# A Pool memset after every fourth gather, in a gather, cumulative sum and projection kernel

## The chip, the cores and the metric

The kernel runs on one core of one Trainium2 chip. The metric is the device time in microseconds (us) of one execution. Medians of several executions are quoted, with the lowest and highest; a profiled execution gives the trace, whose span is 1.7 to 1.8 us shorter than the measured time of the same execution. A ratio is the mean time of one kernel's fast runs over the mean of the other's fast runs of the same rounds, so it is not quite the ratio of the medians quoted. A run counts as fast when it lies within 1.5% of the fastest run of its kernel.

In the lines of the profile PE is TensorE, PEld its weight loads, DVE VectorE, ACT ScalarE, POOL the GpSimd engine (Pool in this text) and SP SyncE. A record is the entry of one instruction in the trace. The landing time of a gather runs from its issue to the arrival of its data.

## The reference

```python
x: (16, 4096, 512) float32;  indices: (16, 2048), sorted, distinct;  w: (512, 512) float32
gathered = x[b_idx, indices, :]
cs = np.cumsum(gathered, axis=1)
return np.matmul(cs, w)            # (16, 2048, 512) float32
```

## The kernel before

The 16 x 2048 gathered rows are worked on as 256 tiles of 128 rows. For each tile the Pool issues one indirect DMA, which reads 128 rows of 2 KB and casts them to float16 on the way. TensorE multiplies the tile with a triangle of ones (four `sums` matmuls), VectorE adds the last row of the tile before (`carry`), TensorE projects with `w` (four `project` matmuls), ScalarE copies to SBUF, and SyncE stores four tiles, 1 MB, at a time. Buffers go round: sixteen gather tiles, four of most others. These are the lines that the change and the argument touch:

```python
    def gather(t):
        g, r = divmod(t, R)                       # R = 2
        if t % FREE == 0:                         # wait until an old gather tile has been summed
            pool.need(s_a, t + FREE - min(NG, 3 * R + max(t // (4 * R), 1) * R))
        ...                                       # ap: 128 row numbers, one per partition
        nc.gpsimd.indirect_dma_start(
            out=g16[g % (NG // R)][:, r, :], out_offset=None, in_=x_flat,
            in_offset=bass.IndirectOffsetOnAxis(ap=ap, axis=0),
            element_offset=(t // NT) * S * D,
        ).then_inc(s_g[t % NS], 16)
    ...
    for t in range(T):                            # T = 256, the whole program of the Pool
        gather(t)                                 # after a few fills at the start
    nc.gpsimd.drain()
    ...
    # in store(g, n): four tiles in one DMA
        nc.sync.dma_start(
            out=rows.rearrange(order, p=P, j=R), in_=src[:, g % W : g % W + n]
        ).then_inc(done, 16)
```

Of the kernel before, what the change touches and what calls it, by code (L numbers as in the profile page):

```python
# [7 lines left out]
P = 128  # L8
FP32 = mybir.dt.float32
FP16 = mybir.dt.float16  # L10
# [23 lines left out]
def kernel(  # L34
# [7 lines left out]
    nc = tc.nc  # L42

    B, S, D = x.shape
# [15 lines left out]
    NB = 4  # L60
# [10 lines left out]
    const = ctx.enter_context(tc.tile_pool(name="const", bufs=1))  # L71
# [10 lines left out]
    ident = const.tile([P, P], FP32)  # L82
    zeros = const.tile([P, D], FP16)
    spare = const.tile([P, 1], FP16)
    g16 = [const.tile([P, R, D], FP16, name=f"g16_{i}") for i in range(NG // R)]
    cst = [const.tile([P, DC, R, P], FP16, name=f"cst{i}") for i in range(NC)]
    ob = [const.tile([P, W, R, D], FP32, name=f"ob{i}") for i in range(NO)]
# [5 lines left out]
    def sem(name):  # L93
        return tc.alloc_semaphore(name)
# [5 lines left out]
    s_w = [sem(f"s_w{c}") for c in range(DC)]  # L100
    s_idx = [sem(f"s_idx{k}") for k in range(KI)]
    s_f = [sem(f"s_f{i}") for i in range(NO)]
    s_ol = sem("s_ol")
    s_g = [sem(f"s_g{i}") for i in range(NS)]
    s_o = [sem(f"s_o{i}") for i in range(NO)]
# [5 lines left out]
    pool, pe, dve, act, sp = (  # L111
        Lane(e) for e in (nc.gpsimd, nc.tensor, nc.vector, nc.scalar, nc.sync)
    )

    def gather(t):
        g, r = divmod(t, R)
        if t % FREE == 0:
            pool.need(s_a, t + FREE - min(NG, 3 * R + max(t // (4 * R), 1) * R))
        if t < FIRST:
            pool.need(s_first[g], 16)  # L120
            ap = idx_first[:, t, 0:1]
        else:
            pool.need(s_prep, t // P + 1)
            ap = idxg[:, t // P, t % P : t % P + 1]
        nc.gpsimd.indirect_dma_start(  # L125
            out=g16[g % (NG // R)][:, r, :],
            out_offset=None,
            in_=x_flat,
# [3 lines that stand above are left out]
# [93 lines left out]
    with nc.allow_non_contiguous_dma(reason="a few indices, one per partition"):  # L225
        for k, eng in enumerate((nc.sync, nc.scalar)):
            t = k * R
# [56 lines left out]
    ).then_inc(s_ut, 1)  # L284
    for t in range(T):
        gather(t)
    nc.gpsimd.drain()  # L287


# [124 lines left out]
```

## Time and profile before

| | value | how to read it |
|---|---|---|
| time | 354.61 us (354.37 to 355.48) | median of 3 runs |
| span of the profiled run | 352.6 us | all trace times count from its start |
| Pool | 69% busy | but 1.245 us from gather to gather, so nearly full |
| gather, issue to landing | 3.7 / 12.7 / 20.8 us | least, median, most: a queue in front of the DMA |
| last gather starts | 324.1 us | 28.5 us before the end of the span |

The lines themselves stand in the prediction.

### The profile page before, as it was taken

Reading aid. Unit: us, or ns where it says so; the run is one execution under the profiler, and the core shown is the slowest. Engines: PE = TensorE matmul, PEld = TensorE weight load, DVE = VectorE, ACT = ScalarE, POOL = GpSimd, SP = SyncE. Lnnn points to the kernel's source line nnn. Section 1 sums busy time; section 2 is a strip of 40 time slices with the busy share of each in tenths; the row PEclk is TensorE's granted clock in tenths of the full one; section 3 lists DMA queues with packets and bytes.
Section 4 is the critical chain, followed back from the end, with each engine's and each line's share of the span. In section 5 each row is a group of like instructions: output and inputs, shape, how many; then the busy total and the mean of one; then the engine's idle time right before and its main releaser. Section 6 shows DMA issues by size and latency. Waiting matters only on the chain.

```text
span 352.6 us, 6043 instructions
## 1 busy us (share of the span) xinstructions
PE 300.1 (85%) x2066; PEld 151.4 (43%) x2066; DVE 179.2 (51%) x263; ACT 152.7 (43%) x260; POOL 242.7 (69%) x266
## 2 busy tenths in 40 slices
PE   7687959889799898889979889889898988998983
PEld 2343525445344444444435444444444534443531
DVE  2554636555455455545546455455555545554531
ACT  2333525435344444444444445354444444444532
POOL 6777777777777777777777777777777767766000
PEclk9999999999999999999999999999999999999998
DMA  7999999999999999999999999999999999999996
GB/s 190 178 225 275 298 245 307 281 304 295 295 312 301 284 315 304 283 312 302 299 297 302 300 297 311 297 291 317 291 299 311 289 302 307 302 299 298 309 319 242
DMA packets 56315, 102.14 MB, mean 290 GB/s; under 512 B 5872, under 2 KB 38896, under 8 KB 56304
## 3 DMA queue, kind: packets, MB, share of 16 engines
q0 software_dynamic: 36864, 33.57, 58.9%
q1 hardware_dynamic: 18880, 67.90, 50.4%
q10 hardware_dynamic: 560, 0.53, 0.4%
q8 instruction: 6, 0.10, 0.1%
q14 instruction: 5, 0.04, 0.0%
HBM read 68.42 MB, written 67.11 MB: 384 GB/s over the span
## 4 chain that ended last, share of the span: by engine, by line
DMA 57%; POOL 23%; PE 9%; issue 9%; POOLq 0%; ACT 0%; SPq 0%
DMA g<-in_x_dram,idxg 56%; POOL g L125 23%; PE pb L190 6%; PE pa L145 3%; DMA idx_first<-in_indices_dram 1%; POOLq L287 0%; ACT ob L202 0%; SPq L409 0%; SPq L91 0%
## 5 line engine op out<-in xcount | busy, mean ns | idle before, releaser
L125 POOL DMA_INDIRECT g<-in_x_dram,idxg x252 | 237.2, 941 | 79.8 <-issue 64.3
L190 PE MATMUL pb<-w,cst 128*128 128x512 f16 x1024 | 262.3, 379 | 0.0
L177 DVE TENSOR_TENSOR cst<-pa,cst 128x512 f16<-128x512 f32 x240 | 166.1, 692 | 150.3 <-PE pa L145 148.5
L202 ACT COPY ob<-pb 128x512 f32<-128x512 f32 x256 | 150.1, 586 | 190.0 <-PE pb L190 190.0
L145 PE MATMUL pa<-ut,g 128*128 128x128 f16 x992 | 97.1, 220 | 43.1 <-DMA g<-in_x_dram,idxg 42.8
L145 PEld LDWEIGHTS pa<-ut,g 128*128 128x128 f16 x992 | 68.3, 98 | 123.6 <-DMA g<-in_x_dram,idxg 92.4
L190 PEld LDWEIGHTS pb<-w,cst 128*128 128x128 f16 x1024 | 89.5, 98 | 61.6 <-issue 0.5
L164 DVE CAST cst<-pa 128x512 f16<-128x512 f32 x16 | 11.1, 692 | 9.9 <-PE pa L145 9.9
L293 PE MATMUL pb<-zeros 128*128 128x512 f16 x16 | 5.7, 519 | 1.5 <-DVE zeros L297 1.5
L125 POOL DMA_INDIRECT g<-in_x_dram,idx_first x4 | 4.0, 989 | 1.6 <-issue 0.9
L145 PE MATMUL pa<-uq,g 128*128 128x128 f16 x32 | 3.1, 220 | 2.3 <-DMA g<-in_x_dram,idx_first 1.3
L145 PEld LDWEIGHTS pa<-uq,g 128*128 128x128 f16 x32 | 2.1, 98 | 4.8 <-DMA g<-in_x_dram,idxg 2.0
L293 PEld LDWEIGHTS pb<-zeros 128*128 128x128 f16 x16 | 1.9, 125 | 4.0 <-issue 2.0
L300 DVE CAST idxf<-idx 128x128 f32<-128x128 uint32 x2 | 0.5, 227 | 4.1 <-DMA idx<-in_indices_dram 4.1
L363 ACT ACT_TABLE_LOAD x1 | 1.3, 1283 | 2.5 <-issue 2.5
L366 ACT CAST w<-w 128x512 f16<-128x512 f32 x2 | 1.1, 614 | 2.6 <-DMA w<-in_w_dram 2.6
L314 DVE CAST w<-w 128x512 f16<-128x512 f32 x2 | 0.8, 451 | 1.2 <-DMA w<-in_w_dram 1.2
L305 PE MATMUL pb<-ident,idxf 128*128 128x128 f32 x2 | 0.7, 374 | 0.3 <-DVE idxf L300 0.3
L305 PEld LDWEIGHTS pb<-ident,idxf 128*128 128x128 f32 x2 | 0.4, 184 | 1.2 <-DVE idxf L300 0.9
L297 DVE MEMSET zeros<- 128x256 uint32 x1 | 0.3, 272 | 1.1 <-SPq L91 1.1
L311 DVE CAST idxg<-pb 128x128 uint32<-128x128 f32 x2 | 0.6, 288 | 0.2 <-PE pb L305 0.2
L253 POOL MEMSET ident<- 128x128 f32 x1 | 0.2, 205 | 0.5 <-SPq L91 0.5
(10 smaller groups left out, 1.9 us busy)
## 6 DMA issues: line engine op xcount, KB each, us to landing
out_dram<-ob SPq DMA_DIRECT2D x59, 1024.0 KB, 8.0
out_dram<-ob SPq DMA_DIRECT2D x8, 512.0 KB, 5.1
g<-in_x_dram,idxg POOLq DMA_INDIRECT x252, 12.8
out_dram<-ob SPq DMA_DIRECT2D x4, 256.0 KB, 3.3
w<-in_w_dram ACTq DMA_DIRECT2D x2, 256.0 KB, 3.7
w<-in_w_dram SPq DMA_DIRECT2D x2, 256.0 KB, 4.5
idx<-in_indices_dram SPq DMA_DIRECT2D x2, 128.0 KB, 3.2
g<-in_x_dram,idx_first POOLq DMA_INDIRECT x4, 4.2
```

The costliest lines, as they stand in the source:

```text
L125: nc.gpsimd.indirect_dma_start(out=g16[g % (NG // R)][:, r, :], out_offset=None, in_=x_flat, in_offset=bass.IndirectOffsetOnAxis(ap=ap, ax ...
L145: mm = nc.tensor.matmul(out=pa[t % NA][:, c], lhsT=g16[g % (NG // R)][:, r, c * P : (c + 1) * P], rhs=uq[:] if g in PLAIN else ut[:], star ...
L164: nc.vector.tensor_copy(out=dst, in_=src).then_inc(s_d, 1)
L177: nc.vector.tensor_tensor(out=dst, in0=src, in1=last, op=mybir.AluOpType.add).then_inc(s_d, 1)
L190: mm = nc.tensor.matmul(out=pb[u % NB][:], lhsT=cst[g % NC][:, c, j, :], rhs=w16[:, c, :], start=(c == 0), stop=(c == DC - 1),)
L202: nc.scalar.copy(out=ob[g // W % NO][:, g % W, j], in_=pb[u % NB][:]).then_inc(s_e, 1)
L293: nc.tensor.matmul(out=pb[NB - 1][:], lhsT=zeros[:, :P], rhs=zeros[:], start=True, stop=True)
L305: nc.tensor.transpose(out=pb[k % NB][:, :P], in_=idxf[:, k, :], identity=ident[:]).then_inc(s_pt, 1)
L311: nc.vector.tensor_copy(out=idxg[:, k, :], in_=pb[k % NB][:, :P]).then_inc(s_prep, 1)
L314: nc.vector.tensor_copy(out=w16[:, c, :], in_=w32[:, c, :]).then_inc(s_wc, 1)
L363: nc.scalar.copy(out=spare[:], in_=zeros[:, :1])
L366: nc.scalar.copy(out=w16[:, c, :], in_=w32[:, c, :]).then_inc(s_wc, 1)
```

## The change

The change is meant to give the Pool one more instruction per four gathers, about as long as a gather instruction, that nobody needs and that no other engine waits for. It shows what the Pool's time is worth in this kernel.

```diff
+    rest = const.tile([P, D * 3 // 2], FP16)
...
+    s_r = sem("s_r")
...
     for t in range(T):
         gather(t)
+        if t % NB == NB - 1:                      # NB = 4
+            pool.need(s_r, t // NB)
+            nc.gpsimd.memset(rest[:], 0.0).then_inc(s_r, 1)
     nc.gpsimd.drain()
```

The wait is for the memset before, four gathers earlier, since all of them write the same tile.

## The prediction

> **What bounds the kernel now.** I read the page of the kernel before first, then the line of the gathers by itself, then the chain that ended last in order of time, and last the Pool's own timeline at both ends of the run. The kernel takes 354.61 us (median); the profiled execution has a span of 352.6 us.
>
> From the page, the engine shares, the slices and the costliest lines:
>
> ```profile
> PE 300.1 (85%) x2066; PEld 151.4 (43%) x2066; DVE 179.2 (51%) x263; ACT 152.7 (43%) x260; POOL 242.7 (69%) x266
> ...
> POOL 6777777777777777777777777777777767766000
> ...
> DMA  7999999999999999999999999999999999999996
> ...
> DMA 57%; POOL 23%; PE 9%; issue 9%; POOLq 0%; ACT 0%; SPq 0%
> ...
> L125 POOL DMA_INDIRECT g<-in_x_dram,idxg x252 | 237.2, 941 | 79.8 <-issue 64.3
> ```
>
> The columns of the last line are busy us, mean ns, and the idle time in front. The Pool reads as 69% busy, but 252 gathers of 0.94 us with 79.8 us of idle in front make 317.0 us: it has almost no room. 64.3 us of that idle is put down to "issue", that is, to nothing the Pool waited for. The timeline in the middle of the run shows it as a fixed 0.30 us in front of each gather (columns: start, length, what, and idle before it):
>
> ```profile
> 156.72 0.94 POOL L125 DMA_INDIRECT g<-in_x_dram,idxg  x1 [0.30 <-issue]
> ...
> 157.97 0.94 POOL L125 DMA_INDIRECT g<-in_x_dram,idxg  x1 [0.30 <-issue]
> ...
> 159.22 0.94 POOL L125 DMA_INDIRECT g<-in_x_dram,idxg  x1 [0.30 <-issue]
> ```
>
> One gather costs the Pool 1.245 us from start to start, so 256 of them 318.8 us. The DMA is a little slower still. The view of the gathers' own line gives waits and landings:
>
> ```profile
>   issue: 65.2, 214
>   PE pa L145: 15.5, 41
> ...
> DMA to landing us min/median/max: 3.7/12.7/20.8
> ```
>
> The 41 waits for buffers total 15.5 us, of which 41 x 0.30 = 12.3 us is the fixed gap that a gather has anyway: only 3.2 us is true waiting. The landing time is the more telling line. The chain in order of time shows it rise all through the run, and the last gather comes last of all (columns: start, length, what):
>
> ```profile
> 12.25 5.50 DMA g<-in_x_dram,idxg
> ...
> 105.64 10.98 DMA g<-in_x_dram,idxg
> ...
> 230.21 16.99 DMA g<-in_x_dram,idxg
> ...
> 324.12 20.75 DMA g<-in_x_dram,idxg
> ```
>
> So the Pool issues at 1.245 us a tile, the DMA engines carry tiles (gather and store together) more slowly, and the difference lies as a queue in front of the DMA. The DMA's pace: first issue at 3.19, last landing at 324.12 + 20.75 = 344.87, so 341.7 us for 256 tiles, 1.335 us each. Pool and DMA are thus within 7% of each other: the DMA is the bound now, and the Pool's slack is 0.09 us a tile, some 0.36 us for four tiles, no more. From the last landing to the end of the span there are 352.6 - 344.87 = 7.7 us of tail (last sums, projection, copy, store).
>
> **What the Trainium skill says.** GPSIMD Engine Reference, section Instruction dispatch, says that each of the eight cores takes the next Pool instruction once its own share of the last is done, with no barrier between instructions. The trace agrees as far as it goes: the four one-element memsets at the start begin 0.03 us apart (0.31, 0.34, 0.37, 0.40) though each record lasts 0.10 to 0.12 us. The same page, section When to use GPSIMD, says that a pair of these cores writes the descriptors of a DMA issued there. Nothing in the trace of before shows which cores work; if it is so, a memset needs those two cores for its partitions too, and comes in series with the gathers on them. Perfetto Trace Analysis, section GPSIMD Engine Instruction, advises timing Pool instructions by the spacing of their starts and not by the reported duration; here that matters, 1.245 against 0.94 us. VectorE: DVE Perf Modes, section Zero memsets can be issued as uint32 (trn2), says that a memset costs a cycle per element whatever the type, and that a zero memset on VectorE may be issued in 4-byte words. The trace agrees: VectorE's zeros row has 128x256 uint32 for 512 halves, and on Pool 128 f16 take about what 128 f32 do.
>
> **The change part by part.** Nothing is removed or moved. Added are 64 Pool memsets of 128x768 f16, one behind each fourth gather, and in front of each (but the first) a wait for the memset before it, which four gathers (5 us) separate from it, so that wait should never hold. Nobody reads the tile; no engine but Pool gets work, and DMA traffic is the same.
>
> The cost of one memset, from these rows of the timeline at the start:
>
> ```profile
> 0.34 0.10 POOL L398 MEMSET const-float32-1.0<- 128x1 f32 x1
> ...
> 1.02 0.20 POOL L253 MEMSET ident<- 128x128 f32 x1 [0.51 <-SPq L91]
> 1.16 0.21 POOL L254 MEMSET ut<- 128x128 f16 x1
> ...
> 1.93 0.20 POOL L274 MEMSET uq<- 128x128 f16 x1
> ```
>
> One element has a record of 0.10 us and 128 elements one of 0.205: 0.105 / 127 = 0.83 ns an element. So 768 elements make 0.64 us and a record of 0.10 + 0.64 = 0.74 us, which is near enough to "about as long as a gather" (0.94). By start spacing, 128 elements hold the Pool for 0.14 us (1.02 to 1.16), that is 0.03 fixed and 0.11 for the elements; 768 then hold it for 0.03 + 0.64 = 0.67 us. Between two gathers the whole 0.67 and perhaps the 0.07 us until its writes are confirmed is added; I take 0.70 us.
>
> What lies beside other work: the Pool's slack of 0.36 us per four tiles is smaller than 0.70, so about half of each memset eats the DMA's queue, and from then on the Pool sets the pace at 1.245 + 0.70 / 4 = 1.42 us a tile, above the DMA's 1.335. The backlog that grows to 20.75 us never forms.
>
> The sum. Start of the first gather 3.19; extra length of the first gather and of the first with the computed indices, 0.19 + 0.15 (records 1.13 and 1.09); 255 periods of 1.245 = 317.5; 63 memsets of 0.70 before the last gather = 44.1. Last gather starts at 365.1. The same sum without memsets gives 320.9, plus 3.2 of buffer waits 324.1, as measured (324.12), which supports it. Those waits should vanish. The last landing with a short queue: the four first gathers took 4.2 us at the median, and some store traffic is beside it, so 6 us as a choice: 371.1. Tail 7.7: 378.8. The measured time stands 2.0 above the span (354.61 - 352.6): 380.8, taken as 381 us.
>
> **The rivals.** First, the memset could hide in the 0.30 us in front of a gather. If those 0.30 us are the sequencer's work for the next gather, and can go on while the cores fill, only 0.40 us a memset is left: 63 x 0.40 = 25.2 in place of 44.1 gives 362, and with a Pool pace of 1.345 a tile the DMA is nearly the bound again, with a longer last landing: 362 to 364. For it: the gap is the same behind a wait and without one. Against it: between two gathers it is not hidden, and where a semaphore released a gather late (317 us and after) about 0.26 us still passed before its record began, so it seems to be part of the gather itself.
>
> Second, the zero could be written in 4-byte words as on VectorE: 384 elements, 0.03 + 0.32 = 0.35 us. That is the slack of 0.36 almost exactly: Pool 1.33 and DMA 1.335 a tile, and the end comes between today's 354.6 and 362; I would say 359. Against it: the page names VectorE only, and a record of 0.42 us would not be "about as long as a gather". The Pool's f16 fills now are of 1.0 and tell nothing of zero.
>
> Third, going back from a fill to descriptor work could cost a new start: the 0.30 us gap after the memset as well as before it, or the 0.19 us by which the first gather was longer. With 0.70 + 0.30 = 1.00 a memset the sum is 18.9 us higher, 400; with 0.19 it is 12 higher, 393. For it: the first gather after the fills at the start is indeed 1.13 us. Against it: the two records there belong to first uses.
>
> Fourth, the DMA stays the bound and nothing changes, if a memset on Pool ran beside the gathers on other cores. The slack needed is 0 to 0.36 us per memset. The page's pair of cores speaks against it.
>
> **Range and chances.** Centre 381 has about six chances in ten (374 to 387, for 0.60 to 0.80 us a memset). The two cheap rivals have together some two in ten and end near 359 to 364; the dear one nearly two in ten, 393 to 400. So 361 to 399 should hold it 8 times in 10. Two per cent is 7.1 us: slower than 361.7 at 0.86, within it 0.13 (mostly the packed fill), faster 0.01.
>
> **What would show it.** Each memset should have a record near 0.74 us and be 128x768 f16; the start spacing of the gathers around it should be 1.245 + 0.70 = 1.95 us; three of four spacings stay at 1.245. The median landing should fall from 12.7 to some 5 to 7 us without a rise over the run; the Pool's waits for sums should be near zero; the chain should name the Pool for most of the span in place of DMA 57%; the DMA slices should drop from nines to a mixture of eights and nines, and the last gather should start near 365. It is wrong if the spacing around a memset is 1.6 (hidden or packed) or 2.2 and over (a new start), or if landings still climb to 20 us.

## The result and the profile after

The changed kernel takes 378.14 us (377.80 to 379.42, 4 runs) against 354.49 us; the ratio is 1.0672, with a 95% interval of 1.0636 to 1.0708. 381 us was predicted.

From the page of the changed kernel: busy time of the engines, the slices of Pool and DMA, the chain that ended last, and the groups of the gathers and memsets (busy us, mean ns, idle time in front):

```profile
PE 300.8 (80%) x2066; PEld 152.4 (41%) x2066; DVE 180.0 (48%) x263; ACT 152.7 (41%) x260; POOL 291.1 (77%) x330
...
POOL 6788788788788888888878878878878878878830
...
DMA  7999999999999999999999999999999999999995
...
POOL 52%; DMA 26%; issue 13%; PE 7%; ACT 0%; POOLq 0%; SPq 0%
...
L127 POOL DMA_INDIRECT g<-in_x_dram,idxg x252 | 237.5, 942 | 68.0 <-issue 62.3
...
L291 POOL MEMSET rest<- 128x768 f16 x64 | 48.5, 758 | 0.0
```

The chain has gone over from DMA (57%) to Pool (52%). The memset is 0.758 us, the gather as long as it was. No idle time stands in front of the memsets, and the gathers have 11.8 us less in front of them than they had.

The Pool's timeline of the changed kernel in the middle of the run (start, length, what, and idle before it):

```profile
157.16 0.94 POOL L127 DMA_INDIRECT g<-in_x_dram,idxg  x1 [0.30 <-issue]
158.41 0.94 POOL L127 DMA_INDIRECT g<-in_x_dram,idxg  x1 [0.30 <-issue]
159.34 0.75 POOL L291 MEMSET rest<- 128x768 f16 x1
160.26 0.95 POOL L127 DMA_INDIRECT g<-in_x_dram,idxg  x1 [0.17 <-issue]
161.51 0.95 POOL L127 DMA_INDIRECT g<-in_x_dram,idxg  x1 [0.30 <-issue]
```

From gather to gather over the memset it is 160.26 - 158.41 = 1.85 us. All 63 such spacings in the trace lie between 1.85 and 1.86; with 1.245 taken off, a memset adds 0.61 to 0.62 us to the Pool. The 0.757 us of its median record are not all added: the gather behind it has a gap of 0.165 us in place of 0.30, so 0.757 + 0.165 - 0.30 = 0.62.

The line of the gathers by itself:

```profile
  issue: 63.3, 232
  PE pa L147: 5.6, 23
...
DMA to landing us min/median/max: 3.2/6.0/7.8
```

The queue is gone. By stretch of the run, the median landing is 5.2 us in the first 40 us, 5.6 up to 100, 6.4 up to 200, 6.0 up to 300 and 6.2 to the end, where the kernel before goes 5.5, 8.4, 12.2, 17.3 and 19.0. The last gather starts at 360.07 us, 36.0 us later than before, but the span grew by 23.5 us only: behind the last gather there are 16.0 us in place of 28.5. Its own landing takes 7.0 us in place of 20.75, and the tail behind that 9.0 us in place of 7.7. So of the 63 x 0.62 = 39 us that the memsets add in front of the last gather, 12.5 us are paid by the queue that never forms, and the buffer waits that vanish (3.2 us before) pay most of the remaining 3.

### The profile page after: what moved, and what is told of

Same layout as the page of the kernel before. It is cut to its first block, busy times and chain, and to the rows that moved or that the text cites. A ratio compares the mean times of both kernels' runs of the same rounds, so it can differ in the third digit from the quotient of the medians.

```text
span 376.1 us, 6107 instructions
## 1 busy us (share of the span) xinstructions
PE 300.8 (80%) x2066; PEld 152.4 (41%) x2066; DVE 180.0 (48%) x263; ACT 152.7 (41%) x260; POOL 291.1 (77%) x330
## 4 chain that ended last, share of the span: by engine, by line
POOL 52%; DMA 26%; issue 13%; PE 7%; ACT 0%; POOLq 0%; SPq 0%
POOL g L127 43%; DMA g<-in_x_dram,idxg 25%; POOL rest L291 9%; PE pb L192 5%; PE pa L147 3%; DMA idx_first<-in_indices_dram 1%; ACT ob L204 0%; POOLq L292 0%; SPq L414 0%; SPq L92 0%
## 5 line engine op out<-in xcount | busy, mean ns | idle before, releaser
L291 POOL MEMSET rest<- 128x768 f16 x64 | 48.5, 758 | 0.0
L319 DVE CAST w<-w 128x512 f16<-128x512 f32 x2 | 1.6, 842 | 1.1 <-DMA w<-in_w_dram 1.1
```

The source lines that it names most:

```text
L291: nc.gpsimd.memset(rest[:], 0.0).then_inc(s_r, 1)
L319: nc.vector.tensor_copy(out=w16[:, c, :], in_=w32[:, c, :]).then_inc(s_wc, 1)
```

## The experiments

Each run is compared with the kernel before on the same chip; all kernels were built from the two shown. The twelve runs fell on four chips. On three of them the kernel before took 355 us; four runs fell on the other, where it took 406 us, and come last.

**Half as wide and twice as wide.** Two runs, on one chip with the two experiments after them:

```diff
-    rest = const.tile([P, D * 3 // 2], FP16)
+    rest = const.tile([P, D * 3 // 4], FP16)     # half_width
+    rest = const.tile([P, D * 3], FP16)          # double_width
```

> The memset is 128x384 f16, half as wide. Theory (the Pool's clock of instructions counts, and the DMA keeps its pace of 1.335 us a tile as a floor): record 0.757 - 0.32 = 0.44 us, the spacing of gathers around a memset 1.86 - 0.32 = 1.54 us, so 1.319 us a tile on Pool, just below the DMA; the time ends near the kernel before, 355 to 360 us, and landings climb to 10 us or more again. Rival 1 (every Pool microsecond adds to the time): halfway, 366 us. Rival 2 (the cost is one per memset, not per column: a start, a wait): 378 us.

Measured: 359.98 us (359.43 to 360.63), kernel before 355.06 us, ratio 1.0136 (1.0101 to 1.0171). The record was 0.437 us and the spacing over a memset 1.54 us. The time is at the upper end of what the theory gave and both rivals miss. But one part of the theory failed: the landings did not climb as they had been expected to. Their median is 8.3 us between 100 and 200 us and 8.2 us behind 300 us. In the line of the gathers:

```profile
DMA to landing us min/median/max: 3.5/7.6/10.3
```

With a gather each (340.3 - 3.3) / 255 = 1.32 us the DMA kept up to the end. So its pace is a little quicker than the 1.335 us that I had worked out: the DMA's time per tile came from first issue to last landing, and so counted the first landing's latency as work; from first landing (3.19 + 4.2 = 7.4) to last (344.87) it is 337.5 / 255 = 1.323 us.

> The memset is 128x1536 f16, twice as wide. Theory (Pool bound, 0.83 ns a column): record 0.757 + 0.64 = 1.40 us, spacing around a memset 2.50 us, last gather at 360.1 + 63 x 0.64 = 400.4, time 416 to 419 us, landings shorter than 6 us. Rival (a fixed cost per memset): 378 to 380 us.

Measured: 418.67 us (417.87 to 419.41), ratio 1.1793 (1.1750 to 1.1836). The record was 1.397 us, the spacing 2.49 to 2.50 us, the last gather started at 400.7, the median landing 5.3 us. Between single and double width the record grows by 0.640 us for 768 columns: 0.83 ns each, the slope that the 1- and 128-element fills had given. The rival of a fixed cost per memset falls.

**Only the instruction.**

```diff
+    rest = const.tile([P, 2], FP16)
```

> The memset is 128x2 f16: only the instruction and its wait are left. Theory: record 0.10 us, spacing around it 1.245 to 1.27 us (its start costs next to nothing), time as the kernel before, 354 to 356 us. Rival (going from a fill back to descriptor work costs a start of 0.15 to 0.3 us whatever the width): spacing 1.4 to 1.55 us; at 0.3 us the time is still within the DMA's slack, so the spacing decides and not the time.

Measured: 355.29 us (354.92 to 355.51), ratio 1.0010 (0.9976 to 1.0044). Its Pool timeline over a memset:

```profile
157.07 0.94 POOL L127 DMA_INDIRECT g<-in_x_dram,idxg  x1 [0.30 <-issue]
157.99 0.13 POOL L291 MEMSET rest<- 128x2 f16 x1
158.32 0.95 POOL L127 DMA_INDIRECT g<-in_x_dram,idxg  x1 [0.19 <-issue]
```

The spacing is 1.25 us, as without a memset: the 0.12 us of the record fits into the gap that the gather has anyway. Neither the instruction nor the wait for the memset before it costs anything measurable, so the rival of a start after each fill falls. Landings climb to 20.5 us as in the kernel before.

**A quarter of the partitions, all columns.**

```diff
-            nc.gpsimd.memset(rest[:], 0.0).then_inc(s_r, 1)
+            nc.gpsimd.memset(rest[:32, :], 0.0).then_inc(s_r, 1)
```

> The memset is 32x768 f16: a quarter of the partitions, the same columns. Theory (each core walks its columns, all partitions together): record 0.75 us, spacing 1.86 us, time 378 us as the changed kernel. Rival (the bytes written count, or their traffic into SBUF): a quarter of 0.64 us, spacing 1.38 us, time 354 to 357 us.

Measured: 378.47 us (378.35 to 378.72), ratio 1.0661 (1.0626 to 1.0696), with a record of 0.757 us for 32x768. A quarter of the bytes costs the same: columns count, and not bytes.

**Fills of the same size on VectorE.** The kernel before, with this in VectorE's program and no fills on the Pool. The value is 1.0 and not 0, so that the fill should stay 768 elements of f16:

```diff
+    def fill(t):
+        if t % NB == NB - 1:
+            nc.vector.memset(rest[:], 1.0)
...
         carry(t)
+        fill(t)                                   # in the head, the loop and the tail
```

> The kernel before with the same 64 fills of 128x768 f16 (of 1.0) issued from VectorE, one after each fourth carry, none on Pool. On a chip where the kernel before takes about 355 us: theory (what costs is time in the Pool's order of instructions, and VectorE has room, 180 of 353 us busy) record about 0.8 us, gathers stay at 1.245 us, 354 to 358 us. Rival (the fill's writes into SBUF[...] disturb the gathers): 370 us and over, with longer gathers or gaps.

Measured: 354.46 us (353.27 to 354.96), ratio 0.9984 (0.9954 to 1.0014). VectorE's busy time rose to 215.3 us; the gathers were as quick as before and their landings climbed as before. The group of the fills, and the landings from the line of the gathers:

```profile
L318 DVE MEMSET rest<- 128x768 f16 x64 | 44.7, 698 | 6.9
...
DMA to landing us min/median/max: 3.6/13.4/20.3
```

So the tile, and writing it from VectorE, cost no time. With the spacing over a memset, this points to the place in the Pool's order as what costs.

**Half of the stores left out**, in the kernel before and in the changed one. The result is wrong: of each stored pair of blocks only the first is sent, and the rest of the output is never written.

```diff
-            out=rows.rearrange(order, p=P, j=R), in_=src[:, g % W : g % W + n]
+            out=rows.rearrange(order, p=P, j=R)[:, : max(n // 2, 1)],
+            in_=src[:, g % W : g % W + max(n // 2, 1)]
```

> The same kernel as half_stores_before, because that run fell on a chip where the kernel before takes 406 us and TensorE, not DMA or Pool, sets the pace. On a chip where the kernel before takes about 355 us: theory (Pool floor without DMA queue) last gather at 321, landings flat at 4 to 5 us, 334 to 339 us; rival (gathers alone set the DMA's pace) landings climb to 20 us, 352 to 355 us. On a chip of 406 us it should stay at 405, as it did.

Measured: 336.22 us (335.82 to 336.60) against 354.66, ratio 0.9477 (0.9460 to 0.9494). The line of the gathers and, from the page, the DMA's slices:

```profile
DMA to landing us min/median/max: 3.7/4.9/8.0
...
DMA  7999999999999999999999999999999999999984
```

With the stores' bytes nearly halved the queue is gone and the last gather starts at 320.9 us, the figure that the sum of 255 spacings gives without any wait. This shows that in the kernel before gathers and stores together made the DMA the slower one, and that the Pool's floor lies 18 us lower. (The cut takes bytes from the DMA engines and from the memory behind them at once; these two are not separated.) It also shows what the DMA slices are worth: nines in both cases, with a queue and without.

> The same kernel as half_stores_after, for the same reason. On a chip where the kernel before takes about 355 us: theory (Pool bound) last gather still near 360, 373 to 377 us; rival (the DMA still counts) 358 to 363 us. On a chip of 406 us it should stay at 404, as it did.

Measured: 374.37 us (374.17 to 375.13), ratio 1.0561 (1.0542 to 1.0580). From the line of the gathers:

```profile
L127 POOL DMA_INDIRECT g<-in_x_dram,idxg x252: 936/938/952, 9.0 to 359.8; - x126
...
DMA to landing us min/median/max: 3.2/4.2/6.4
```

The last gather starts at 359.8 us, nearly as with all the stores. Of the 18.4 us that the same cut saved the kernel before, it saves the changed kernel 378.1 - 374.4 = 3.8 us (runs of different rounds), nearly all behind the last gather. The DMA no longer sets the pace. The two half-store kernels ran on one chip in the same rounds, and between them the memsets cost 374.37 - 336.22 = 38.2 us, against 24 us with all the stores: without a queue that could pay, the time rises by nearly the whole 63 x 0.62 = 39 us.

**A wait for the memset's completion** in front of the next gather:

```diff
             nc.gpsimd.memset(rest[:], 0.0).then_inc(s_r, 1)
+            pool.need(s_r, t // NB + 1)
```

> The same kernel as completion_wait, whose trace showed 0.27 us between memset and gather in place of 0.165, on a chip where TensorE set the pace and the time told nothing. On a chip where the kernel before takes about 355 us: theory (Pool bound, 0.11 us more for each memset) spacing 1.97 us, last gather 63 x 0.11 = 7 us later than 360.1, 383 to 387 us. Rival (the wait is hidden elsewhere): 378 us.

Measured: 384.54 us (383.81 to 385.13), ratio 1.0830 (1.0805 to 1.0856). The last gather starts at 366.6 us, 6.5 us later than in the changed kernel. From its Pool timeline:

```profile
155.56 0.94 POOL L127 DMA_INDIRECT g<-in_x_dram,idxg  x1 [0.30 <-issue]
156.50 0.75 POOL L291 MEMSET rest<- 128x768 f16 x1
157.52 0.95 POOL L127 DMA_INDIRECT g<-in_x_dram,idxg  x1 [0.27 <-POOL rest L291]
```

The gap behind the memset is 0.27 us, and the spacing 1.96 us. So without the wait there is an overlap of the memset's last stretch with the preparation of the next gather, worth about 0.1 us, and the wait takes it away: 63 x 0.105 = 6.6 us. Which part of which of the two overlaps, and how much of the 0.105 us is the delay of the semaphore itself, is not settled by this.

**The four runs on the slower chip.** There the kernel before took 406.01 us (405.02 to 407.91), and the mean granted clock of TensorE in its runs was 0.940 to 0.974, against 0.987 to 0.994 in its runs beside half_width, where it took 355. completion_wait is the same kernel as completion_wait_2.

> The kernel before, with only the first half of each paired store sent (part of the output is left unwritten on purpose, so the result is wrong). Theory (before, gathers and stores together keep the DMA just slower than the Pool): with about half the store bytes the DMA is ahead, landings stay near 4 to 5 us all through, the last gather starts at 320.9 and the time is 334 to 339 us, the Pool's own floor. Rival (the gathers alone set the DMA's pace, the stores ride along): landings still climb to 20 us, 352 to 355 us.

> The changed kernel with the same half of the stores (wrong on purpose). Theory (Pool bound): the last gather still starts at 360.1; only the last landing and the tail get shorter, 373 to 377 us against 378. Rival (the DMA still counts, the memsets only add to it): it falls as much as the kernel before does, by 15 to 20 us, to 358 to 363.

> The changed kernel, in which the gather after a memset waits for that memset's completion. Theory (the next gather's preparation and the memset's last stretch overlap by the 0.14 us that 0.757 + 0.165 - 0.30 falls short of the record): with the wait the overlap is gone, the memset's record is followed by 0.28 to 0.35 us, spacing 1.97 to 2.05 us in place of 1.86, last gather 7 to 12 us later, 385 to 390 us. Rival (there is no overlap, the record of the memset just starts early or ends late): spacing stays 1.86 to 1.90, 378 to 380 us.

> The changed kernel with four memsets in a row after each 16 gathers. Theory (the sum of Pool time counts, and 16 tiles build no queue that could bridge the pause): memsets start 0.67 us apart, each group adds 0.62 + 3 x 0.67 = 2.63 us, 15 groups before the last gather 39.5 against 38.9 us, 377 to 381 us. Rival (a queue in front of the DMA bridges the pauses, so rarer and longer ones are hidden): 360 to 370 us.

The edit of four_together:

```diff
-        if t % NB == NB - 1:
-            pool.need(s_r, t // NB)
-            nc.gpsimd.memset(rest[:], 0.0).then_inc(s_r, 1)
+        if t % (4 * NB) == 4 * NB - 1:
+            for k in range(4):                    # rest is [P, 4, 768] here
+                pool.need(s_r, t // (4 * NB) * 4)
+                nc.gpsimd.memset(rest[:, k], 0.0).then_inc(s_r, 1)
```

Measured, in the order of the texts above: 405.90 us (404.62 to 405.99; ratio 0.9992), 404.38 us (403.96 to 405.62; ratio 0.9973), 410.99 us (409.22 to 411.40; ratio 1.0113) and 427.57 us (426.42 to 427.95; ratio 1.0527). As times they miss what each theory gave. From the page of half_stores_before on this chip, the granted clock by slice and the chain:

```profile
PEclk9989969989999998999999998999999998989999
...
PE 77%; issue 10%; DVE 6%; another core or an unknown queue 4%; DMA 1%; ACT 0%; POOL 0%; DVEq 0%; SPq 0%
```

On this chip the chain names TensorE for 77%, and a cut of the stores or the 64 memsets with it change the time by 0.3% at most. (That last comparison is of half_stores_after with the unchanged kernel; the changed kernel itself was not run there.) So the price of a memset found above holds only where no other engine is slower than Pool and DMA. The memsets in fours cost 5% there; the granted clock was lowest in that kernel, 0.877 to 0.905 over its runs, against 0.925 to 0.974 in the others there, but that the pauses lower the clock is only a guess. Why this chip took 51 us longer is open; no trace of the kernel before was kept there. The half-store kernel was traced on both chips: TensorE is busy 318.2 us there and 300.5 us here, 18 us more, while the span is 404.3 against 334.7 us. So the larger part is idle time between its instructions, and a lower clock that only makes them longer does not explain that.

The Pool's own records do agree with the theory even there: the gap behind the memset was 0.27 us in completion_wait; and in four_together four memsets took 2.79 us together, so they started (2.79 - 0.757) / 3 = 0.68 us apart, and the gather behind them began 3.89 us after the one in front, 2.65 us more than without (2.63 expected). Whether rarer, longer pauses cost the same in time as single ones, on a chip where the Pool sets the pace, was not tried again.

One more question stays open: why the gather comes behind the memset. The prediction took it that the memset needs the cores that write the descriptors. No run confined a fill to other partitions than theirs, so none separates that from plain order of instructions.

## Why the prediction was right

The time, 378.14 us, lies in the range (361 to 399) and 2.9 us from the centre; slower was the likeliest class. All times behind the points below are from traces; this table sums up where the end lies:

| kernel | last gather starts | end of span | between |
|---|---|---|---|
| before | 324.1 | 352.6 | 28.5 |
| tiny | 325.3 | 353.4 | 28.1 |
| half_width | 340.3 | 358.9 | 18.6 |
| changed | 360.1 | 376.1 | 16.0 |
| completion_wait_2 | 366.6 | 383.4 | 16.8 |
| double_width | 400.7 | 417.0 | 16.3 |
| half_stores_before_2 | 320.9 | 334.7 | 13.8 |
| half_stores_after_2 | 359.8 | 372.6 | 12.8 |

- **The bound before.** Right: the DMA, with the Pool close behind. half_stores_before_2 shows both. The size of the Pool's slack was a little too large: with the DMA at 1.323 us a tile it is 4 x 0.078 = 0.31 us for four tiles and not 0.36.
- **The record of the memset.** 0.74 predicted, 0.757 measured, unpacked, as 128x768 f16. The packed rival falls by the record.
- **What a memset adds.** 0.70 predicted, 0.62 measured, the largest error. The spacing over it was 1.85 to 1.86, not 1.95. The mechanism, that the memset comes in series with the gathers, was right; its size was not. The prediction took 0.67 us for holding the Pool and 0.03 more as a part of the 0.07 us until the writes are confirmed. The 0.67 is what one memset holds the next back (0.68 in four_together), but between two gathers the memset adds 0.06 us less than that, and nothing of the 0.07 comes on top. Only when the gather is made to wait for the memset, in completion_wait_2, are 1.96 - 1.245 = 0.72 us added, about what was predicted. The first rival, that the memset hides in the gap of 0.30, was right for about 0.14 us of its record. The 0.08 us too much make 63 x 0.08 = 5 us: last gather 365.1 predicted, 360.1 measured.
- **Behind the last gather.** 6 + 7.7 = 13.7 us predicted, 16.0 measured: 7.0 for the last landing and 9.0 of tail. The chain shows the gather before the last three, issued at 356.32, land 7.59 us later, and TensorE then work without a pause from 363.97 to 370.40. The last four tiles land within 3.2 us (363.9 to 367.1), and TensorE is behind them: it starts on the last at 368.26, 1.2 us after its landing. The tail of 7.7 was taken from a kernel in which TensorE was waiting for the last tile when it landed. half_stores_after_2, with 12.8 us, shows that the stores still in flight make about 3 us of the 16.
- **The sum.** 5.0 us too much in front of the last gather and 2.3 too little behind it leave 2.7 us of error. That the total is closer than its larger part is luck: the two errors have opposite signs. The 2.0 us between span and time compare a median with the span of another execution; within one execution it is 1.7 (377.8 - 376.1, and 354.26 - 352.6 before). Taken in the same way, the result has 2.0 too, so no error comes of it.
- **The signs named.** The chain went to the Pool, the landings fell to 6.0 us without a rise, and the 23 waits for sums (5.6 us) are, with 0.24 us each, no more than the gap a gather has anyway. One sign was wrong: the DMA slices stay at nines. The experiments show why it was a poor sign.
- **The dear rival**, a new start after each fill, falls with tiny.

## What to carry to other kernels

When two resources run within a few per cent of each other, work out the pace of each per tile, and compare what is added to the difference: here half of the memset's width (0.30 us per four tiles against 0.31) cost 1.4%, and from single to double width the further 0.64 us cost their full length (40.5 us for 63 of them). In a kernel like this one, judge the slower of the two by the time from issue to landing along the run, and by the spacing of starts, since neither the busy share of the Pool (69% when nearly full) nor the DMA slices (nines with and without a queue) tells it. Filler work belongs to an engine off the chain: here 64 fills on VectorE cost nothing measurable, on the Pool 24 us.

## What the Trainium skill lacked or had wrong

- GPSIMD Engine Reference has no duration for a memset on the Pool. Here: a record of 0.116 us for 2 columns, 0.437 for 384, 0.757 for 768 and 1.397 for 1536, which is 0.83 ns a column, with the same record for 32 and 128 partitions at 768 columns; four in a row start 0.68 us apart.
- The same page has nothing on how much a gather overlaps the instruction in front of it. Here 0.30 us stand between two gathers, 0.165 us between a memset and a gather, and 0.27 us when the gather waits for the memset's semaphore.
- DMA: Bandwidth & Descriptors, section Anatomy of one DMA — SWDGE (gpsimd) path, calls descriptor generation "small, variable" among the parts of one DMA's fixed time, and does not say how long the Pool is held when gathers follow each other. Here it is 1.245 us from start to start for 128 rows, which is 94% of the 1.323 us that the DMA takes for a tile, gather and store together. How much of the 1.245 us is descriptor generation, no run here separates.
- VectorE: DVE Perf Modes, section Zero memsets can be issued as uint32 (trn2), leaves open what happens to a zero memset on the Pool. Here it ran as 128x768 f16, not packed.
